# A hybrid decoder layer on one core: the down projection as seven products of halves

## The chip, the core and the metric

The kernel runs on one core of a Trainium2 chip. The core has five engines with queues of their own: TensorE (PE: matmuls, and weight loads, PEld), VectorE (DVE), ScalarE (ACT), GpSimd (POOL) and SyncE (SP), which issues the DMA transfers here. The metric is the device time of one execution in microseconds. The kernel before has a median of 2500.06 us over three runs (2499.16 to 2500.68).

## What is computed

One layer (DEPTH = 1) over 16 meta tokens and 1024 tokens, D_MODEL = 1024, all in float32: a token mixer (attention, a state-space mixer, gates), a norm, a gated MLP with a short convolution, and a last norm. The change touches only the end of the MLP:

```python
def conv_glu_ffn(h, w_up, conv_w, conv_b, w_down):
    u = causal_dwconv(h @ w_up, conv_w, conv_b)
    gate, val = jnp.split(u, 2, axis=-1)
    return (jax.nn.silu(gate) * val) @ w_down        # [1024 tokens, 2816] @ [2816, 1024]
...
ffn = conv_glu_ffn(h, w_up[i], ffn_conv_w[i], ffn_conv_b[i], w_down[i])
h = layer_norm(DEEPNORM_ALPHA * h + ffn, ln2_g[i], ln2_b[i])
```

## The kernel before

Every product of two float32 matrices is made of three float32r matmuls: `split` (L197) cuts a tile x into a high part H (a cast on ScalarE, L198) and a rest L (a subtraction on VectorE, L199), and H·H, L·H and H·L are added up in PSUM.

The kernel goes through its stages one after the other: embedding norm and latents, attention, output projections and gates, the state-space mixer, the mixer's output with the first norm, the up projection (L1083 to L1221), the down projection with the last norm (L1224 to L1308). The order on each queue is fixed when the kernel is built, by a planner that gives each engine the ready instruction that stands earliest in the program; `tc.high_priority(n)` lets instructions count as n places earlier (400 from L652 on). Tiles come from pools; a new tile waits until the tile whose place it takes is done with. SBUF is handed from stage to stage in this way, and each engine's queue runs in its order: an instruction that waits holds up all behind it.

Up projection (loop over f at L1178, 22 blocks of 128 hidden channels for gate and value): it already uses Strassen's seven products in Winograd's form, over halves of channels and of tokens. `wrest` (L1100) loads up weights (`wraw`), forms four sums s1 to s4 on GpSimd (L1107 to L1110) and splits them; `first` starts the next block's first product while the present one runs. Each product is 24 matmuls of 258 and 256 columns into a pair of banks (`dpair`). Results are combined on VectorE and ScalarE (L1191 to L1217), go through `conv_up` (L1127; `va`, `ga`, `gb` are its tiles, and two of its instructions, L1132, run on VectorE with two inputs), are multiplied and stored to DRAM as `gv_d[f]`, the second half of the tokens first (L1216, L1220).

Down projection: two halves r of 512 tokens. In each, `load_r` loads eight residual tiles `hr` and scales them on ScalarE (L1257, L1258), and the 22 channel blocks k go in groups (`KBLK`, L91: 2, 4, 4, 4, 4, 4). For each k `load_d` loads a whole row block of `w_down` (512 KB) into `wraw`, two buffers, and splits it into two column halves (`wh`, `wl`, 12 buffers of each); `load_g` loads `gv_d[k]` for this half of the tokens (256 KB) into `gv`, three buffers, and splits it into `dh` tiles, which have room for all of r. So `w_down` is loaded and split twice. Four token tiles t have two PSUM banks each, eight in all; the residual comes into PSUM by transposes with `ident` (L1296), ahead of the first group's matmuls. The matmuls of a group run tile by tile (L1305):

```python
for k in range(k0, k1):
    dhh, dhl = dh[k][0][:, o], dh[k][1][:, o]
    for i in range(3):
        for q in range(2):
            wh, wl = wd[k][q]
            a, b = ((dhh, wh), (dhl, wh), (dhh, wl))[i]
            nc.tensor.matmul(pss[q], a, b, start=False, stop=(k == NFF - 1 and i == 2))
if k1 == NFF:
    norm2(pss, 512 * r + P * t)
```

`norm2` (L1262) runs wholly on VectorE: `bn_stats` over the two banks (L1265), `bn_aggr` (L1267), nine small instructions for the inverse root (L234 to L239), then two instructions for each half (L1273, L1275), and two stores of `yt`.

## Time and profile before

| | us |
|---|---|
| median of three runs | 2500.06 |
| the profiled execution: its time | 2499.16 |
| its span, first to last instruction | 2497.2 |
| TensorE busy | 2412.9 (97%) |
| VectorE busy | 1675.0 (67%) |
| ScalarE busy | 1111.7 (45%) |
| GpSimd busy | 168.5 (7%) |
| last up matmul, first down matmul | 2224.43, 2236.82 |

Times in the trace count from the start of the span. Matmuls overlap in the pipeline, so the mean duration of one is longer than the step from one to the next; a step is found by dividing a full stretch by the matmuls in it. An idle time in brackets or behind a bar is that of the engine just before the instruction, with what ended it. The chain is followed back from the last instruction, at each step to what released it. The granted clock of TensorE has two levels, 2.4 GHz (1.00) and 1.2 GHz (0.50); a stretch's number is the mean.

### The profile page before, as it was taken

To read this page: it belongs to the slowest core of one execution; us is meant where nothing else is said; L and a number is where in the kernel's file an instruction comes from. 1 tells how busy PE (TensorE), PEld (TensorE's weight loads), DVE (VectorE), ACT (ScalarE), POOL (GpSimd) and SP (SyncE) were. 2 spreads that over 40 slices of the span, in tenths; PEclk is the share of its full clock that TensorE was granted. 3 is DMA by queue.
4 is the path that set the end of the run, shared out by engine and by line. 5 is a ranking of instruction groups with operands and counts; after the bars stand their busy time and mean duration, and the time that the engine had idled before them with its cause. 6 is when DMAs were issued, how large, how long until landed. Compare 5 with 4: busy or idle time off the path is not lost.

```text
span 2497.2 us, 42526 instructions
## 1 busy us (share of the span) xinstructions
PE 2412.9 (97%) x16451; PEld 2279.8 (91%) x16451; DVE 1675.0 (67%) x3834; ACT 1111.7 (45%) x2436; POOL 168.5 (7%) x168
## 2 busy tenths in 40 slices
PE   6999999999999999999999999999789999989998
PEld 6998898889999999999999999999789999987886
DVE  6467677774667777877777646746787777755624
ACT  6345455562245455545554323423544444445211
POOL 0000000000000000000000001001332222200000
PEclk9999999999999999999999999999899999999999
DMA  5121111152552212213222445534222222257421
GB/s 203 47 66 35 36 38 32 51 154 72 171 187 91 94 62 87 86 62 99 75 79 67 136 149 169 194 129 142 99 90 77 77 77 77 77 172 247 155 93 68
DMA packets 113530, 257.10 MB, mean 103 GB/s; under 512 B 13488, under 2 KB 48560, under 8 KB 111280
## 3 DMA queue, kind: packets, MB, share of 16 engines
q1 hardware_dynamic: 113328, 254.38, 31.3%
q8 instruction: 129, 2.11, 0.4%
q14 instruction: 73, 0.60, 0.1%
HBM read 200.97 MB, written 51.26 MB: 101 GB/s over the span
## 4 chain that ended last, share of the span: by engine, by line
PE 83%; DVE 7%; DMA 4%; ACT 2%; issue 1%; POOL 1%; SPq 0%; DVEq 0%; ACTq 0%; POOLq 0%
PE d L191 24%; PE g L171 12%; PE g L173 12%; PE g L172 12%; PE c L1305 7%; PE c L605 3%; PE c L880 2%; PE c L904 1%; PE c L599 1%; PE c L884 1%; DMA yl<-y_d 1%; DMA gv<-gv_d 1%; DVE f L199 1%; PE c L552 1%; PE c L554 1%
## 5 line engine op out<-in xcount | busy, mean ns | idle before, releaser
L191 PE MATMUL d<-f,wh 128*128 128x258 f32 (+1 forms) x4000 | 656.5, 287 | 22.6 <-ACT c L1159 5.8
L191 PEld LDWEIGHTS d<-f,wh 128*128 128x128 f32 x4000 | 560.5, 193 | 26.0 <-ACT c L1159 6.0
L171 PE MATMUL g<-h,wh 128*128 128x348 f32 (+3 forms) x1560 | 506.7, 325 | 4.0 <-ACT lat L387 4.0
L173 PE MATMUL g<-h,wh 128*128 128x348 f32 (+3 forms) x1560 | 505.6, 325 | 0.0
L172 PE MATMUL g<-h,wl 128*128 128x348 f32 (+3 forms) x1560 | 505.4, 324 | 0.0
L191 PE MATMUL d<-f,wl 128*128 128x258 f32 (+1 forms) x2000 | 407.0, 286 | 5.7 <-DVE wl L199 4.1
L191 PEld LDWEIGHTS d<-f,wl 128*128 128x128 f32 x2000 | 314.8, 193 | 7.2 <-DVE wl L199 5.0
L171 PEld LDWEIGHTS g<-h,wh 128*128 128x128 f32 x1560 | 293.9, 188 | 7.0 <-ACT lat L387 4.4
L161 DVE TENSOR_TENSOR wl<-wraw,wh 128x512 fp32r<-128x512 f32 (+2 forms) x278 | 192.4, 694 | 160.3 <-ACT wh L160 157.2
L172 PEld LDWEIGHTS g<-h,wl 128*128 128x128 f32 x1560 | 294.3, 189 | 2.5 <-issue 2.4
L173 PEld LDWEIGHTS g<-h,wh 128*128 128x128 f32 x1560 | 293.8, 188 | 2.4 <-issue 2.4
L160 ACT CAST wh<-wraw 128x512 fp32r<-128x512 f32 (+2 forms) x278 | 166.9, 604 | 251.7 <-PE d L191 119.0
L199 DVE TENSOR_TENSOR wl<-wraw,wh 128x512 fp32r<-128x512 f32 x154 | 111.5, 750 | 150.6 <-ACT wh L198 106.6
L1305 PE MATMUL c<-wh,dh 128*128 128x512 f32 x704 | 193.1, 396 | 9.4 <-ACT dh L198 8.4
L198 ACT CAST wh<-wraw 128x512 fp32r<-128x512 f32 x154 | 90.7, 618 | 221.5 <-PE c L1305 97.8
L1305 PEld LDWEIGHTS c<-wh,dh 128*128 128x128 f32 x704 | 132.4, 189 | 40.6 <-ACT dh L198 8.7
L171 PE MATMUL g<-a,wh 128*128 128x348 f32 (+2 forms) x456 | 149.2, 327 | 2.0 <-DVE kn L199 1.1
L172 PE MATMUL g<-a,wl 128*128 128x348 f32 (+2 forms) x456 | 147.8, 324 | 0.0
L173 PE MATMUL g<-a,wh 128*128 128x348 f32 (+2 forms) x456 | 147.7, 324 | 0.0
L785 DVE SCALAR_TENSOR_TENSOR xc<-g,V,xc 128x347 f32<-128x347 f32 (+2 forms) x180 | 103.7, 576 | 38.5 <-ACT xc L781 35.6
L870 ACT ACTIVATE G<-ac,tok 116x116 f32<-116x116 f32 x288 | 91.6, 379 | 42.7 <-PE c L880 42.7
L1305 PE MATMUL c<-wl,dh 128*128 128x512 f32 x352 | 109.9, 393 | 0.0
(270 smaller groups left out, 3897.8 us busy)
## 6 DMA issues: line engine op xcount, KB each, us to landing
wraw<-win SPq DMA_DIRECT2D x65, 512.0 KB, 3.4
wraw<-wup SPq DMA_DIRECT2D x48, 512.0 KB, 3.5
wraw<-wdl SPq DMA_DIRECT2D x44, 512.0 KB, 3.8
ac<-cs_d SPq DMA_DIRECT2D x16, 1044.0 KB, 5.7
wraw<-wos SPq DMA_DIRECT2D x32, 512.0 KB, 3.9
gv<-gv_d SPq DMA_DIRECT2D x44, 256.0 KB, 4.2
yl<-y_d SPq DMA_DIRECT2D x32, 257.0 KB, 3.5
wraw<-wout SPq DMA_DIRECT2D x16, 512.0 KB, 3.8
```

Of the source, the lines that this page charges most:

```text
L160: nc.scalar.copy(h[:, :n * ncol], r)
L161: nc.vector.tensor_sub(l[:, :n * ncol], r, f32(h[:, :n * ncol]))
L171: nc.tensor.matmul(ps, ah, bh, start=(k == 0), stop=False)
L172: nc.tensor.matmul(ps, al, bh, start=False, stop=False)
L173: nc.tensor.matmul(ps, ah, bl, start=False, stop=(k == n - 1))
L191: nc.tensor.matmul(ps[:, PO + c0:PO + c1], a, b[:, c0:c1], start=(start and k == 0 and i == 0), stop=(k == n - 1 and i == 2), skip_group_c ...
L198: nc.scalar.copy(H, src)
L199: nc.vector.tensor_sub(L, src, f32(H))
L605: nc.tensor.matmul(ops[:, o0:n], vt[j][:w, hh * P:(hh + 1) * P], ptt[:w, o0:n], start=(j == 0), stop=(j == nbmax - 1))
L785: nc.vector.scalar_tensor_tensor(t[:, l:n], ps[:, hal + l - s:hal + n - s], vec("cw", (3 - s) * 24 + ct), t[:, l:n], ALU.mult, ALU.add)
L870: nc.scalar.activation(G_[:, k * S:(k + 1) * S], ac[:S, hh, C0[b] + k * S:C0[b] + (k + 1) * S], AF.Relu, bias=tok[:, 3 * b + k, 32 + hd:33 ...
L1305: nc.tensor.matmul(pss[q], a, b, start=False, stop=(k == NFF - 1 and i == 2))
```

## The change

The down projection becomes seven products too. With A the 1024 tokens by 2816 channels cut into halves of tokens (first digit) and of channels (second), and B = `w_down` cut into halves of channels (`j` and `j + KH`, KH = 11) and of columns, each product is [512 x 1408] times [1408 x 512]: 11 channel blocks, four token tiles, three matmuls of 512 columns each.

- In the up projection `down_sums(j)` is called at the top of the passes f = 4 to 14. It loads two row blocks of `w_down` into `tw1` and `tw2` (one buffer each), forms the right operands of products 7, 5, 4 and 6 with four GpSimd subtractions in place, and stores them to DRAM (`t13_d`, `t42_d`). It has no priority of its own.
- In the down projection `left` gives the left operand: tiles of `gv_d`, loaded once and kept (`raw`, 4 tiles in pool `Ea`, 40 in `Eb`), or sums of them on GpSimd (11 for product 7, 22 for product 6, 11 for product 3). `right` loads a half row block (256 KB) of `w_down` or of a stored sum, two halves sharing one `wraw` tile. `forms` splits both; it has places for seven pairs at a time (4 in `Eh0` and `wp`, 3 in `Eh1` and `Ew`), and in the last product the last seven take places of `Eb`.
- The products go in the order 1, 2, 7, 6, 5, 3, 4, in groups of 4, 4, 3 blocks (the last one 4, 7), into four banks each. Between them results are copied out on ScalarE (`p1`, `u2`, `u4`) or added on VectorE.
- The residual is brought in by four calls of `residual` (four tiles each, 16 transposes), the first of them into banks of its own that ScalarE copies to `u4`.
- `norm2` runs on tiles of SBUF or PSUM. For a half in `pooled` the scaling is a ScalarE activation and two GpSimd instructions in place of two on VectorE: both halves of all tiles after product 3, one half of the first three tiles after product 4, none in the last tile.

```diff
+    t13_d = [dtile(f"t13_d{k}", [P, D]) for k in range(KH)]
+    t42_d = [dtile(f"t42_d{k}", [P, D]) for k in range(KH)]
...
+    def down_sums(j):
+
+        x, y = (pe[0].tile([P, D], F32, name=k, tag=k) for k in ("tw1", "tw2"))
+        nc.sync.dma_start(x, wdl[j])
+        nc.sync.dma_start(y, wdl[j + KH])
+        (b11, b12), (b21, b22) = ((t[:, :512], t[:, 512:]) for t in (x, y))
+        nc.gpsimd.tensor_sub(b11, b12, b11)
+        nc.gpsimd.tensor_sub(b12, b22, b12)
+        nc.gpsimd.tensor_sub(b22, b22, b11)
+        nc.gpsimd.tensor_sub(b21, b21, b22)
+        nc.sync.dma_start(t13_d[j], x)
+        nc.sync.dma_start(t42_d[j], y)
+
...
     for f in range(NFF):
         q = st[f]
+        if f >= NHEAD and f < NHEAD + KH:
+            down_sums(f - NHEAD)
...
+        def left(q, j):
+            if q in (1, 2, 4):
+                return A({1: 11, 2: 12, 4: 22}[q], j)
+            if q == 7:
+                t = p.tile([P, 512], F32, name="s3", tag="s3", bufs=3)
+                nc.gpsimd.tensor_sub(t, A(11, j), A(21, j))
+                return t
+            if q == 6:
+                nc.gpsimd.tensor_add(A(21, j), A(21, j), A(22, j))
+                nc.gpsimd.tensor_sub(A(11, j), A(21, j), A(11, j))
+                return A(11, j)
+            if q == 5:
+                return A(21, j)
+            nc.gpsimd.tensor_sub(A(12, j), A(12, j), A(11, j))
+            return A(12, j)
...
+        def forms(q, j, late):
             with tc.high_priority(wprio[0]):
...
+                n = count[0] % 7
+                res = []
+                for k, src in enumerate((left(q, j), right(q, j))):
+                    if late:
+                        hl = [pb.tile([P, 512], F32R, name="gv", tag="gv") for _ in range(2)]
+                    elif k == 0:
+                        hl = [(ph0 if n < 4 else ph1).tile([P, 512], F32R, name="dh", tag="dh") for _ in range(2)]
+                    else:
+                        pl, b = (wp, 4) if n < 4 else (p, 3)
+                        hl = [pl.tile([P, 512], F32R, name=t, tag=t, bufs=b) for t in ("wh", "wl")]
+                    split(*hl, src)
+                    res.append(hl)
+                count[0] += 1
+            return res
...
+        def product(q, pss, first, before=None, after=None):
+            blocks = ((0, 4), (4, KH)) if q == 4 else ((0, 4), (4, 8), (8, KH))
+            for k0, k1 in blocks:
+                fs = [forms(q, j, q == 4 and k0) for j in range(k0, k1)]
+                for t in range(4):
+                    o = slice(P * t, P * t + P)
+                    if k0 == 0 and before:
+                        before(t)
+                    for j, ((ah, al), (bh, bl)) in zip(range(k0, k1), fs):
+                        for i, (a, b) in enumerate(((ah, bh), (al, bh), (ah, bl))):
+                            nc.tensor.matmul(pss[t], a[:, o], b, start=(first and j == 0 and i == 0),
+                                             stop=(j == KH - 1 and i == 2), skip_group_check=not first)
+                    if k1 == KH and after:
+                        after(t)
...
+                if q in pooled:
+                    nc.scalar.activation(y, parts[q], AF.Identity, bias=nw, scale=rs)
+                    nc.gpsimd.tensor_tensor(y, y, g2[:, f], ALU.mult)
+                    nc.gpsimd.tensor_tensor(y, y, b2[:, f], ALU.add)
...
+        x0 = banks(gtile)
+        rp = banks(ctile)
+        add = residual(1, 1, rp, True)
+        for t in range(4):
+            add(t)
+            nc.scalar.copy(u4[t], rp[t])
+        product(1, x0, True, None, lambda t: nc.scalar.copy(p1[t], x0[t]))
...
+        product(2, x1, False, add, lambda t: nc.vector.tensor_add(p1[t], p1[t], x1[t]))
+        x2 = banks(ctile)
+        product(7, x2, True)
+        product(6, x0, False, None, lambda t: nc.scalar.copy(u2[t], x0[t]))
...
+        product(5, x0, False, None, c22)
+        add = residual(0, 1, x0, False)
+        product(3, x0, False, add, lambda t: norm2(0, t, (p1[t], x0[t]), (), (0, 1)))
+        add = residual(1, 0, x2, False)
...
+        product(4, x2, False, add, c21)
```

## Rows read from the trace of the kernel before

**Rows 1.** The page: busy time of TensorE; the chain's shares by engine.

```profile
PE 2412.9 (97%) x16451; PEld 2279.8 (91%) x16451; DVE 1675.0 (67%) x3834; ACT 1111.7 (45%) x2436; POOL 168.5 (7%) x168
...
PE 83%; DVE 7%; DMA 4%; ACT 2%; issue 1%; POOL 1%; SPq 0%; DVEq 0%; ACTq 0%; POOLq 0%
```

**Rows 2.** Stretches, from the up projection on: length, busy time per engine.

```profile
core 0: us, PE busy (x) PEld busy (x) DVE busy (x) ACT busy (x) POOL busy (x), PEclk, DMA share, GB/s
1782.00:1861.00 79.00, 66.43 (x481) 64.02 (x482) 63.41 (x80) 30.59 (x47) 28.64 (x20) 0.91 0.24 81
1861.00:2200.00 339.00, 338.94 (x2805) 338.59 (x2805) 260.96 (x339) 165.49 (x269) 88.28 (x64) 1.00 0.26 82
2224.50:2236.80 12.30, 3.87 (x35) 3.58 (x34) 6.68 (x12) 5.94 (x11) 0.00 (x0) 0.87 0.61 199
2236.80:2298.00 61.20, 60.23 (x253) 48.20 (x253) 30.84 (x48) 30.52 (x54) 0.00 (x0) 0.97 0.76 251
...
2374.00:2470.00 96.00, 96.00 (x420) 78.38 (x419) 20.71 (x32) 18.29 (x32) 0.00 (x0) 1.00 0.25 80
```

**Rows 3.** Groups by shape from 2224 on: busy us, mean ns | idle before.

```profile
L1305 PE MATMUL c<-wh,dh 128*128 128x512 f32 x704 | 193.1, 396 | 9.4 <-ACT dh L198 8.4 <-ACT wh L198 0.9
...
L199 DVE TENSOR_TENSOR wl<-wraw,wh 128x512 fp32r<-128x512 f32 x84 | 54.1, 688 | 98.0 <-ACT wh L198 54.0 <-PE c L1305 43.5
L198 ACT CAST wh<-wraw 128x512 fp32r<-128x512 f32 x84 | 47.9, 617 | 126.2 <-PE c L1305 97.8 <-DMA wraw<-wdl 27.4 <-DVE wl L199 0.9
```

**Rows 4.** TensorE's timeline at the seam: start, length, instructions [idle before].

```profile
2224.67 3.70 PE L1296 MATMUL c<-K,hr 128*128 128x128 f32 x32
2236.82 2.07 PE L1305 MATMUL c<-wh,dh 128*128 128x512 f32 x4 [8.45 <-ACT dh L198]
2238.69 1.05 PE L1305 MATMUL c<-wl,dh 128*128 128x512 f32 x2
```

**Rows 5.** The chain at the seam: start, length, what.

```profile
2228.37 0.70 DVE ga L1219
...
2230.49 4.97 DMA hr<-h_d
...
2235.57 0.63 ACT hr L1258
2236.20 0.58 ACT dh L198
```

**Rows 6.** GpSimd's groups, 1876 to 2200: first two of four, 63 operations together.

```profile
L1110 POOL TENSOR_TENSOR s<-wraw,s 128x512 f32<-128x512 f32 x16 | 25.9, 1621 | 1.3
L1107 POOL TENSOR_TENSOR s<-wraw 128x512 f32<-128x512 f32 x16 | 20.7, 1293 | 47.9 <-DVE wl L199 47.9
```

**Rows 7.** VectorE, 1876 to 2200: one line's min/median/max, then groups by shape.

```profile
L1132 DVE SCALAR_TENSOR_TENSOR va<-u,V,va x64: 743/941/1670, 1877.2 to 2191.9; 128x512 f32<-128x512 f32 x64
...
L1132 DVE SCALAR_TENSOR_TENSOR va<-u,V,va 128x512 f32<-128x512 f32 x64 | 71.2, 1113 | 15.3 <-ACT va L1130 14.2
...
L199 DVE TENSOR_TENSOR wl<-wraw,wh 128x512 fp32r<-128x512 f32 x48 | 41.7, 870 | 45.5 <-ACT wh L198 45.5
...
L1132 DVE SCALAR_TENSOR_TENSOR gb<-d,V,gb 128x512 f32<-128x512 f32 x32 | 24.0, 750 | 0.5
```

**Rows 8.** One tile's instructions: min/median/max ns, first and last start.

```profile
L700 SPq DMA_DIRECT2D xx<-dt_d x3: 450/478/482, 554.5 to 628.8; - x3
...
L684 ACT ACTIVATE ga<-g x24: 449/451/463, 569.4 to 717.2; 128x334 f32<-128x334 f32 x8, 128x348 f32<-128x348 f32 x8, 128x344 f32<-128x344 f32 x8
```

**Rows 9.** The page's DMA issues: count, size, median us to landing.

```profile
wraw<-wdl SPq DMA_DIRECT2D x44, 512.0 KB, 3.8
...
gv<-gv_d SPq DMA_DIRECT2D x44, 256.0 KB, 4.2
```

**Rows 10.** The chain at the end: start, length, what.

```profile
2482.27 1.22 DVE bs L1265 x2
...
2488.16 1.22 DVE bs L1265 x2
```

More of the change, by code (lines that the diff above doesn't have):

```diff
@@ L90 @@
 NHEAD = 4
-KBLK = ((0, 2), (2, 6), (6, 10), (10, 14), (14, 18), (18, 22))
+KH = NFF // 2
 G_ATT = 3
@@ new lines, in tile_hybrid, with A, right, residual @@
+    cut_psum(4)
+    with pool("Er", 4) as pr, pool("Ea", 4) as pa_, pool("Eh0", 8) as ph0, pool("Eb", 40) as pb, \
+            pool("Eh1", 6) as ph1, pool("Ew", 1) as p:
+        raw = {}
+        count = [0]
+        wr = [None]
+        def A(i, j):
+            if (i, j) not in raw:
+                t = raw[i, j] = (pa_ if i == 11 and j < 4 else pb).tile([P, 512], F32, name="gv", tag="gv")
+                o = 0 if i < 20 else 512
+                nc.sync.dma_start(t, gv_d[j + (KH if i % 10 == 2 else 0)][:, o:o + 512])
+            return raw[i, j]
+        def left(q, j):
[13 more added lines that the diff above has]
+            return A(12, j)
+        def right(q, j):
+            d, o = {1: (wdl[j], 0), 2: (wdl[j + KH], 0), 3: (wdl[j + KH], 512), 4: (t42_d[j], 0), 5: (t13_d[j], 0),
+                    6: (t42_d[j], 512), 7: (t13_d[j], 512)}[q]
+            if count[0] % 2 == 0:
+                wr[0] = wp.tile([P, D], F32, name="wraw", tag="wraw", bufs=2)
+            t = wr[0][:, 512 * (count[0] % 2):][:, :512]
+            nc.sync.dma_start(t, d[:, o:o + 512])
+            return t
+        def forms(q, j, late):
+            with tc.high_priority(wprio[0]):
+                n = count[0] % 7
[12 more added lines that the diff above has]
+            return res
+        def residual(hi, fh, pss, first):
+            with tc.high_priority(wprio[0]):
+                hr = []
+                for k in range(4):
@@ new lines, in residual @@
+            return lambda t: [nc.tensor.matmul(pss[t][:, k * P:k * P + P], hr[k][:, P * t:P * t + P], ident,
+                                               start=(first and k == 0), stop=(k == 3), is_transpose=True,
+                                               skip_group_check=not first) for k in range(4)]
+        def product(q, pss, first, before=None, after=None):
[12 more added lines that the diff above has]
+                        after(t)
@@ L1264, in norm2, with btile @@
+        def btile(name):
+            return [p.tile([P, 512], F32, name=name, tag=name, bufs=4) for _ in range(4)]
+        p1, u2, u4 = btile("p1"), btile("u2"), btile("u4")
+        bs = [[p.tile([P, 2, 6], F32, name="bs", tag="bs", bufs=8) for _ in range(4)] for _ in range(2)]
+        def norm2(hi, t, parts, have=(), pooled=()):
+            bt = bs[hi][t]
             for q in range(2):
-                nc.vector.bn_stats(bs[:, q], pss[q])
+                if q not in have:
+                    nc.vector.bn_stats(bt[:, q], parts[q])
@@ L1266, in norm2 @@
             mv = p.tile([P, 4], F32, name="mv", tag="mv", bufs=2)
[L1267 removed]
+            nc.vector.bn_aggr(mv[:, :2], bt.rearrange("p a b -> p (a b)"))
             rs, ve, nw = (p.tile([P, 1], F32, name=nm, tag=nm, bufs=2) for nm in ("rs", "ve", "nw"))
             rsqrt_col(rs, mv[:, 1:2], LN_EPS, ve, nw, P)
[L1270 to L1271 removed]
+            r0 = 512 * hi + P * t
@@ L1272, in norm2 @@
+            if pooled:
+                nc.vector.scalar_tensor_tensor(nw, mv[:, 0:1], -1.0, rs, ALU.mult, ALU.mult)
             for q in range(2):
-                nc.vector.scalar_tensor_tensor(yt[:, hv_[q]], pss[q], mv[:, 0:1], g2[:, hv_[q]], ALU.subtract, ALU.mult)
-            for q in range(2):
-                nc.vector.scalar_tensor_tensor(yt[:, hv_[q]], yt[:, hv_[q]], rs, b2[:, hv_[q]], ALU.mult, ALU.add)
-                nc.sync.dma_start(out[r0:r0 + P, hv_[q]], yt[:, hv_[q]])
+                f = slice(512 * q, 512 * q + 512)
+                y = p.tile([P, 512], F32, name="yt", tag="yt", bufs=3)
+                if q in pooled:
+                    nc.scalar.activation(y, parts[q], AF.Identity, bias=nw, scale=rs)
+                    nc.gpsimd.tensor_tensor(y, y, g2[:, f], ALU.mult)
+                    nc.gpsimd.tensor_tensor(y, y, b2[:, f], ALU.add)
+                else:
+                    nc.vector.scalar_tensor_tensor(y, parts[q], mv[:, 0:1], g2[:, f], ALU.subtract, ALU.mult)
+                    nc.vector.scalar_tensor_tensor(y, y, rs, b2[:, f], ALU.mult, ALU.add)
+                nc.sync.dma_start(out[r0:r0 + P, f], y)
@@ L1278, in tile_hybrid, with banks @@
+        def banks(tile_):
+            return [tile_() for _ in range(4)]
+        x0 = banks(gtile)
[5 more added lines that the diff above has]
+        product(1, x0, True, None, lambda t: nc.scalar.copy(p1[t], x0[t]))
         g2 = p.tile([P, D], F32, name="g2")
```

70 lines of the change are left out of this document (11 added, 59 removed).

## The prediction

> **What bounds the kernel now.** I read the page's busy shares and chain first [rows 1]: TensorE is busy 97% of the span and carries 83% of the chain, so the number of matmuls is the first thing to price. Then one table of stretches [rows 2], because an average over the whole span hides where TensorE waits. It shows four kinds of time. From 1782 to 1861 us (the first tiles of the up projection) TensorE is idle 12.6 of 79 us at a clock of 0.91 and VectorE is busy 80%: here other engines set the pace. From 1861 to 2200 TensorE is full, VectorE 77%, GpSimd 26%, DMA 26%. At the seam between up and down projection (2224.5 to 2236.8) TensorE does 3.87 us of work in 12.3. In the down projection it is full again: 420 matmuls in 96.00 us, 0.2286 us each. From 2236.8 to 2298 it runs only 253 where 61.2 us would hold 268, with the DMA at 0.76 of its time and 251 GB/s. The waits at the seam come from the chain and TensorE's timeline [rows 4, 5], the prices of single operations from the groups by shape [rows 3, 6, 7].
>
> **Matmuls removed.** Before: 2 halves x 4 tiles x 22 blocks x 3 x 2 = 1056 matmuls of 512 columns; the 704 with a high part as stationary operand are there [rows 3], and half as many have the rest. After: 7 products x 11 blocks x 4 tiles x 3 = 924 of the same shape (a 128x128 stationary piece of the left operand, 512 columns of weights moving, a new stationary load for each). 132 x 0.2286 = **-30.2 us**, all on the path. The transposes of the residual stay 64: four calls of 16.
>
> **The seam.** TensorE did its last up matmul and 32 transposes by 2228.4, then sat idle 8.45 us; the first matmuls after that went at half clock, 1.2 of 2.4 GHz (4 in 2.07, 2 in 1.05 us) [rows 4]. The chain [rows 5] says why: SyncE stood behind the store of the last up tile (L1219, L1220), then loaded residual for the second half (`hr`) before the first `gv` block, and ScalarE scaled that residual before it cut `dh`. Over 2236.8 to 2298 another (268 - 253) x 0.2286 = 3.4 us is lost, half clock included [rows 2]. The change holds four `gv` tiles in a pool of their own (`Ea`) beside four `hr` tiles, so the first block of four can be cut before the up projection ends, and gives 40 further tiles to the rest; the old stall of 8.45 + 3.4 = **-11.9 us** goes. What is late next: the `gv` loads no longer wait for one of three buffers. 40 x 256 KB = 10.5 MB become ready within some 15 us; at 251 GB/s for a share of 0.76, thus 330 GB/s for all of it, that is 32 us of transfer. Weight halves issued behind them wait. The first block covers 48 x 0.2286 = 11 us. A half behind a third of them takes 11 us instead of the 4.2 of such a load [rows 9] and is just covered; behind all, some 20 us are not. Bounds 0 and +20; I take **+5**, since half of these loads can run in the last 15 us of the up projection, where the DMA is at about a quarter.
>
> **Forms.** Each product needs 22 splits (11 left, 11 right): 22 x 0.617 = 13.6 us of ScalarE and 22 x 0.688 = 15.1 us of VectorE [rows 3] in 132 x 0.2286 = 30.2 us; 154 splits against 132 before. There is room on average; the tight place is the ring of seven forms. Where a block of four follows a block of four, the fourth form's buffers come free three matmuls into the last tile of the old block and are needed nine matmuls into the new: 9 + 9 matmuls, 4.1 us, for two casts and two subtractions (2.6 us in a row). That happens six times. Bounds: 0, and 2.3 us each (the chain hidden by almost nothing) = +14; I take **+4**, nearer to nothing, as 420 matmuls ran without a gap in the old ring [rows 2]. Copies out of PSUM wait for a bank used again at least 6 us later (nine matmuls for each of three tiles), so they lie beside matmuls.
>
> **Sums for the right operands.** 11 calls, each two 512 KB loads, four GpSimd operations, two 512 KB stores. GpSimd: 44 x 1.293 to 1.621 us [rows 6] = 57 to 71 us; its queue is 26% busy, so its own time is hidden. The transfers are 23 MB; over 140 us, the shortest that the calls can take (below), they add 165 GB/s to 82, which makes a share of 0.78, about what was reached at 251 GB/s [rows 2]. SyncE takes four more instructions a call, and a store waits for GpSimd with the loads of up weights queued behind it; those go a tile ahead, so I give that no price of its own. What isn't free is VectorE. Operations with two SBUF inputs grow beside GpSimd: `va` has 0.743 at best, 1.113 on average and 1.670 at worst, `wl<-wraw` 0.870 against 0.688, while `gb`, whose source is PSUM, stays at 0.750 [rows 3, 7]. 64 x 0.363 + 48 x 0.182 = 32.0 us for 63 GpSimd operations: 0.51 us each on average, at most 0.92. So 44 sums take 22 us of VectorE, at most 40.
>
> The Trainium skill (GPSIMD Engine Reference, 4.1 Engine selection) sends two-input elementwise work to VectorE, about twice as fast, and so speaks against these sums. The rows agree with the ratio (1.293 against 0.688); on VectorE they would cost it 30 us instead of 22, so little is won by the place, and the total would hardly change.
>
> Where they fall decides. A load written late in the program runs early when its engine is free: the `xx` loads of `dt_chain`, called after three `gate` calls, are issued at 554.5, before the first gate's result at 569.4 [rows 8]. So I expect the calls to run ahead, one per 13 us (3.8 load [rows 9], 5.5 sums, about 4 store), from 1782 on: six calls, 24 sums, before 1861, where VectorE is 80% busy and TensorE waits for it. 24 x 0.51 = 12 us, half of it on the path: **+6 us**. The other five fall where VectorE has 23% free. Bounds: 0 (all beside work) and 24 x 0.92 = +22. A gain is excluded: nothing of the up projection is removed.
>
> **The last norm.** Product 3's tiles are normed under product 4. In product 4 a tile comes each 21 x 0.2286 = 4.8 us; VectorE took 5.9 a tile before (2488.16 back to 2482.27) [rows 10] and now leaves two operations of 0.75 to ScalarE and GpSimd. The last tile stays on VectorE: one addition from PSUM more, one `bn_stats` less, then the old chain from 2488.16 on. Bounds -1 and +4 (a ring of three `yt` tiles held by a store); I take **+0.5**.
>
> **Sum.** -30.2 - 11.9 + 5 + 4 + 6 + 0.5 = -26.6. The profiled execution took 2499.16 us (span 2497.2), 0.9 below the median. 2499.16 - 26.6 + 0.9 = 2473.5; I round to **2473 us**.
>
> **Rivals.**
> (a) Everything hidden: the seam, the ring and the sums cost nothing. -42.1, so 2458 us. For it: TensorE without a gap from 1861 to 2200. Against: three new supplies would all have to be in time. Chance 0.14.
> (b) A starved start: the burst of `gv` loads delays the weights of the first products. Forecast + 15 = 2488 us. For it: 0.76 of the DMA in that stretch already with three buffers. Chance 0.12.
> (c) No change: the ring loses 1.5 us at each of its 19 block joints instead of 4 in all (28), beside the start: 2473 + 24 = 2497. Against: splits use half of VectorE's time. Chance 0.04.
> (d) Slower: GpSimd holds VectorE back. There are 110 new GpSimd operations: 44 sums in up, 44 left operands (11 + 22 + 11), 22 in the norms. At the worst loss seen, 0.92 us, that is 101 us of VectorE. It decides from the point where 46 of them (42 us) land on the path at that price; with two thirds of all, 67 us, the time is 2500 - 42 + 67 = 2525 us. Against it: in the down projection VectorE needs some 155 us (154 x 0.688 and about 50 for copies, statistics and norms) of 225, and 66 x 0.92 still fits. Chance 0.05.
> The Trainium skill (SBUF — State Buffer, Who interferes with whom) has the harder rule that the later of the two is blocked for a whole instruction; by it the sums before 1861 would cost 24 x 1.3 = 31 us, half on the path, and the time would be about 2483. That lies inside (b); the rows show 0.51, not 1.3, on average.
>
> **How the numbers follow.** Forecast 0.65, from 2463 to 2484; (a) 0.14, (b) 0.12, (c) 0.04, (d) 0.05. Leaving out (c), (d) and the far parts of (a) and (b), the range is 2456 to 2489. 0.2%, 5 us, is about what a measurement of this kernel can tell from no change: faster 0.91, same 0.04, slower 0.05.
>
> **What would show it.** Right: 924 matmuls of 512 columns at 0.229; TensorE's idle time at the seam below 3 us and no half clock there; GpSimd's sums beginning before 1800; `va` and `wl` longer before 1930. Wrong: TensorE waiting on `wh` or `wl` at every block (the ring), on `wraw` in the first two products (b), or GpSimd as the releaser of the casts in products 7 and 6, where 33 of its operations (43 us or more) feed 61 us of matmuls.

## The result, and the profile of the changed kernel

The changed kernel takes 2528.85 us (median of four runs, 2526.93 to 2531.04), the kernel before 2499.61 beside it: 1.0119 times as long, 95% interval 1.0101 to 1.0137. The forecast was 2473 us, so the prediction is wrong in sign: 29 us slower where 27 faster were expected. The profiled execution took 2531.04 us, its span is 2529.3, thus 32.1 more than before's.

First the page of the changed kernel: busy times and the chain's shares, as in [rows 1].

```profile
PE 2403.9 (95%) x16319; PEld 2269.6 (90%) x16319; DVE 1745.5 (69%) x3857; ACT 1136.7 (45%) x2481; POOL 336.8 (13%) x278
...
PE 78%; DVE 7%; POOL 4%; DMA 4%; issue 3%; ACT 2%; SPq 0%; DVEq 0%; POOLq 0%; ACTq 0%
```

TensorE has 132 matmuls less and 9 us less work, but it fills only 95% of the span, and GpSimd, with a seventh of TensorE's work, holds 4% of the chain where it had 1%. Cuts of the span at matmuls tell where the time went. The group `d<-f` of L191 has 6000 matmuls in either kernel, the mixer's output and then the up projection; its 2500th, at some 1775 us, comes early in the up projection and ahead of the first load of `down_sums`, which the changed kernel issues at 1781.5. The other cuts are the last of these 6000 and the first and last matmul of the down projection (before: L1305, after: L1321):

| us | before | changed | difference |
|---|---|---|---|
| start to the 2500th of the 6000 matmuls | 1775.6 | 1774.4 | -1.2 |
| from there to the last of them (up projection) | 449.0 | 485.3 | +36.3 |
| from there to the first down matmul | 12.3 | 5.5 | -6.8 |
| down projection, first to last matmul | 250.0 | 243.8 | -6.2 |
| last matmul to the end | 10.3 | 20.2 | +9.9 |

Together 32.1 us, within a rounding. Two stretches of the changed kernel's up projection, as in [rows 2], then the second of them in the kernel before:

```profile
1782.00:1861.00 79.00, 64.81 (x435) 61.77 (x436) 60.96 (x69) 26.51 (x43) 54.47 (x35) 0.85 0.55 191
1861.00:2000.00 139.00, 118.34 (x904) 116.95 (x903) 100.59 (x113) 52.17 (x87) 73.59 (x50) 0.93 0.47 165
...
1861.00:2000.00 139.00, 138.94 (x1150) 138.74 (x1150) 108.27 (x141) 68.27 (x111) 38.19 (x28) 1.00 0.25 80
```

The sums run from 1785 to 1957: they begin where it was foreseen, but a call takes 16 us instead of 13. Before 1861 TensorE runs 46 matmuls less than before (435 after 481 [rows 2]), after it 246 less (904 after 1150). At 139 / 1150 = 0.121 us each that is some 6 us and some 30. From 1861 to 2000 TensorE is idle 20.7 of 139 us and its clock falls to 0.93, where it was full before. No engine is full: VectorE has 72%, GpSimd 53%, the DMA 47%. GpSimd, ScalarE and VectorE wait for each other in turn and for loads, and the chain of that stretch (start, length, what) names them:

```profile
1880.73 0.32 SPq L1233
...
1881.15 5.24 DMA tw<-wdl
...
1886.52 1.73 POOL tw L1184
...
1889.62 1.74 POOL s L1109
1891.35 1.70 POOL tw L1186
1893.06 1.69 POOL s L1110
1894.75 1.25 POOL tw L1187
1896.00 1.26 POOL s L1112
1897.27 5.92 DMA wraw<-wup
...
1903.22 0.63 ACT wh L198
...
1904.48 1.76 DVE wl L199
...
1907.91 1.70 DVE va L1134
```

It is read from the bottom: VectorE waits for ScalarE's cast, that for an up weight (`wraw<-wup`). This load could not be issued before 1897.27, the moment in which `s4` (L1112) is done: `wraw` has two buffers, and GpSimd's sums are the last to read one. `s4` is late because in GpSimd's queue the sums of up weights (L1109 to L1112) stand between those of down weights (`tw`), and the first of these stood until its load, 5.24 us long, had landed. That load in turn stood on SyncE behind the store of `gb` (L1233), which waits for VectorE. Meanwhile TensorE ran out of weights.

The forms of the down projection: GpSimd's groups from 2290 to 2420, and the longest wait from 2300 to 2385 (total, times, longest).

```profile
L1264 POOL TENSOR_TENSOR gv<-gv 128x512 f32<-128x512 f32 x11 | 18.1, 1651 | 11.1 <-DMA gv<-gv_d 10.8
L1265 POOL TENSOR_TENSOR gv<-gv 128x512 f32<-128x512 f32 x11 | 17.9, 1640 | 0.4
L1269 POOL TENSOR_TENSOR gv<-gv 128x512 f32<-128x512 f32 x11 | 16.3, 1490 | 0.2
L1261 POOL TENSOR_TENSOR s<-gv 128x512 f32<-128x512 f32 x9 | 13.2, 1477 | 12.2 <-DVE dh L199 8.7 <-DMA gv<-gv_d 3.5
...
ACT dh L198 <- POOL s L1261: 34.8, 7, 12.2
```

Casts wait 34.8 us for product 7's sums (L1261): between them GpSimd has those of products 6 and 3 (L1264, L1265, L1269) in its queue, and each takes 1.48 to 1.65 us. Product 7 takes 46.3 us instead of 30.2.

And the end of the changed kernel: a group of VectorE after 2484, and two waits there.

```profile
L238 DVE SCALAR_TENSOR_TENSOR nw<-rs,ve 128x1 f32<-128x1 f32 x21 | 8.0, 388 | 0.5
...
ACT yt L1348 <- DVE nw L1343: 22.6, 4, 6.3
POOL yt L1349 <- ACT yt L1348: 10.5, 4, 3.3
```

The same group in the kernel before, from 2470 on:

```profile
L238 DVE SCALAR_TENSOR_TENSOR nw<-rs,ve 128x1 f32<-128x1 f32 x12 | 2.6, 220 | 0.4
```

The norms of product 3 are still under way when product 4's begin. VectorE's part grows beside GpSimd's, even the instructions on 128x1 (mean 388 ns after 220), and what is left to GpSimd waits for ScalarE, and ScalarE for VectorE.

### The profile page after: what moved, and what is told of

Read it like the earlier page. It is cut to its first block, busy times and chain, and to the rows that moved or that the text cites. A ratio compares the mean times of both kernels' runs of the same rounds, so it can differ in the third digit from the quotient of the medians.

```text
span 2529.3 us, 42622 instructions
## 1 busy us (share of the span) xinstructions
PE 2403.9 (95%) x16319; PEld 2269.6 (90%) x16319; DVE 1745.5 (69%) x3857; ACT 1136.7 (45%) x2481; POOL 336.8 (13%) x278
## 4 chain that ended last, share of the span: by engine, by line
PE 78%; DVE 7%; POOL 4%; DMA 4%; issue 3%; ACT 2%; SPq 0%; DVEq 0%; POOLq 0%; ACTq 0%
PE d L191 21%; PE g L171 12%; PE g L173 12%; PE g L172 12%; PE g L1321 5%; PE c L607 3%; PE c L882 2%; PE c L906 1%; PE c L601 1%; PE c L886 1%; DMA yl<-y_d 1%; DMA tw<-wdl 1%; DVE f L199 1%; PE c L554 1%; PE c L556 1%
## 5 line engine op out<-in xcount | busy, mean ns | idle before, releaser
L191 PE MATMUL d<-f,wh 128*128 128x258 f32 (+1 forms) x4000 | 666.5, 289 | 44.5 <-ACT u L1219 9.1
L191 PEld LDWEIGHTS d<-f,wh 128*128 128x128 f32 x4000 | 569.1, 196 | 49.6 <-ACT wh L198 10.3
L191 PE MATMUL d<-f,wl 128*128 128x258 f32 (+1 forms) x2000 | 412.0, 289 | 5.2 <-DVE wl L199 3.6
L191 PEld LDWEIGHTS d<-f,wl 128*128 128x128 f32 x2000 | 319.6, 196 | 6.6 <-DVE wl L199 4.4
L199 DVE TENSOR_TENSOR wl<-wraw,wh 128x512 fp32r<-128x512 f32 x136 | 119.0, 884 | 74.3 <-ACT wh L198 74.3
L198 ACT CAST wh<-wraw 128x512 fp32r<-128x512 f32 x136 | 82.4, 618 | 120.6 <-DMA wraw<-wup 60.5
L1134 DVE SCALAR_TENSOR_TENSOR va<-u,V,va 128x512 f32<-128x512 f32 x88 | 99.9, 1135 | 20.9 <-ACT va L1132 19.5
L1321 PE MATMUL g<-wh,dh 128*128 128x512 f32 x352 | 112.4, 401 | 1.5 <-ACT wh L198 1.5
```

The lines of the kernel that those rows point to most:

```text
L191: nc.tensor.matmul(ps[:, PO + c0:PO + c1], a, b[:, c0:c1], start=(start and k == 0 and i == 0), stop=(k == n - 1 and i == 2), skip_group_c ...
L198: nc.scalar.copy(H, src)
L199: nc.vector.tensor_sub(L, src, f32(H))
L1134: nc.vector.scalar_tensor_tensor(t, src[:, 2 - k:HN - k], vec("fw", (2 - k) * 44 + ti), t, ALU.mult, ALU.add)
L1321: nc.tensor.matmul(pss[t], a[:, o], b, start=(first and j == 0 and i == 0), stop=(j == KH - 1 and i == 2), skip_group_check=not first)
```

## The experiments

Three suspects, one for each loss; in the up projection also the question whether GpSimd's work, its traffic or its place in the queues costs the time. Lengths in this section come from one profile each, at the cuts of the table above; times of whole runs carry their intervals. The runs were taken in groups, with the kernel before beside each: 2497.57 us for n1 to n4, 2500.85 for n5 to n8, 2498.07 for n9 to n11, 2498.96 for n12. A difference of whole times across groups is uncertain by up to 3 us, so small ones rest on the lengths. Where an expectation gives the up projection 781, 817 or 827 us, it counts from the first of the 6000 matmuls; here it counts from the 2500th: 449.0 us before, 485.3 in the changed kernel.

### The up projection

**n1_down_alone** leaves out the sums of the down weights; the products that took them take raw halves.

```diff
-            down_sums(f - NHEAD)
...
-            d, o = {... 4: (t42_d[j], 0), 5: (t13_d[j], 0), 6: (t42_d[j], 512), 7: (t13_d[j], 512)}[q]
+            d, o = {... 4: (wdl[j + KH], 0), 5: (wdl[j], 0), 6: (wdl[j + KH], 512), 7: (wdl[j], 512)}[q]
```

> Left out: all of down_sums (no loads, no GpSimd subtractions, no stores of the 11 pairs); the four products that took sums of down weights take raw halves of w_down instead, in the same loads of the same size, so the output is not the reference's. Everything else is the change: seven products with their left-operand sums on GpSimd, and the last norm. Both theories of the up projection (the queues that SyncE and GpSimd share, or the port that GpSimd and VectorE share) expect the up projection to end where it did before, at 2224 us of the span (after: 2260), so 36 us sooner, and a time near 2529 - 36 = 2493 us. A third theory, that the two up-projection losses are due to something else in the change (other placement of the buffers, another order from the planner), expects an end of the up projection above 2240. Seam, product 7 (46 us) and the tail of 20 us after the last matmul stay as in the changed kernel if those losses have nothing to do with the sums of the down weights.

Measured: 2496.18 us, 0.9992 of the kernel before (0.998 to 1.0005). The up projection takes 448.6 us and ends at 2226.5. Product 7 (46.1) and the end (19.9) are as in the changed kernel. So all of the 36 us come from `down_sums`, and the rest of the change, with 30 us of matmuls removed, gains nothing by itself.

**n2_sums_no_dma** keeps the 44 GpSimd operations, on one resident pair of tiles, and leaves out the other loads and the stores. It also holds each group of four behind the `s4` of the block's up weights.

```diff
+            if f == NHEAD:
+                with tc.issue_after(st[f - 1]["ga"]):
+                    tw = down_loads(0)
+            with tc.issue_after(st[f]["s4"]):
+                down_sums(*tw)
```

> Left out: the loads of w_down into tw and the stores of the sums, except one pair of loads; the 11 x 4 GpSimd subtractions run as in the change, but on one resident pair of tiles, each group right behind that pass's own sum s4 on GpSimd. The products of the down projection take raw halves of w_down, so the output is not the reference's. It keeps GpSimd's work (44 operations of 1.2 to 1.7 us) and takes away its traffic. Port theory (a GpSimd operation that reads on-chip memory holds VectorE's operations back, 0.5 to 0.9 us for each): 44 x 0.5 to 0.9 = 22 to 40 us of VectorE in a stretch where it has 25 us to spare, so an end of the up projection at 2235 to 2260 us. Queue theory (loads of up weights wait on SyncE behind stores that wait for GpSimd; GpSimd waits for loads): end at 2224 to 2232 us, time near 2493 to 2500.

Measured: 2505.15 us (1.0028, 1.0016 to 1.004); up projection 457.5 us, end at 2232.8, between the two theories' numbers. Its chain decides: the 8.5 us are lost between the 3000th and the 3500th matmul, where the only call with loads stands and two more run close behind it.

```profile
1868.44 4.79 DMA tw<-wdl
...
1873.30 1.19 POOL tw L1186
...
1882.32 1.26 POOL s L1112
1883.59 3.45 DMA wraw<-wup
```

A `tw` load, GpSimd's queue, `s4`, an up weight. From the 3500th matmul on, with most calls still to come, 2000 matmuls take 242.2 us against 241.5 before. So GpSimd's work as such was not the cause of the 36 us.

**n3_dma_no_sums** keeps the 22 loads and 22 stores where the planner had put them and leaves out the four subtractions.

```diff
-        nc.gpsimd.tensor_sub(b11, b12, b11)
-        nc.gpsimd.tensor_sub(b12, b22, b12)
-        nc.gpsimd.tensor_sub(b22, b22, b11)
-        nc.gpsimd.tensor_sub(b21, b21, b22)
```

> Left out: the four GpSimd subtractions of each down_sums; its two loads and two stores stay, placed by the planner as in the change, so t13 and t42 hold raw halves and the output is not the reference's. It keeps the traffic (22 loads and 22 stores of 0.5 MB) and takes GpSimd's work away. Queue theory with GpSimd as a link of it (stores wait for sums, up-weight loads wait behind stores): without the sums a store waits only for its load, 4 us, so about half of the 36 us goes, an end of the up projection at 2235 to 2250 us. Theory that the traffic alone does it: end at 2255 to 2260 as in the changed kernel. Port theory: end at 2224 to 2230, as nothing is left of its cause.

Measured: 2502.52 us (1.0022, 1.0009 to 1.0034); up projection 455.4 us, end at 2234.9, the lower edge of what the queue theory gave. The traffic alone, bunched as it is without sums between, costs 6.4 us; the stretch where it falls:

```profile
1782.00:1861.00 79.00, 64.38 (x452) 61.79 (x451) 58.29 (x81) 32.87 (x52) 23.62 (x17) 0.88 0.70 236
```

The DMA works at 0.70 there (before: 0.24, [rows 2]). 8.5 us by the sums (one call's loads among them) and 6.4 by the traffic make 15 of 36; the rest needs both.

**n4_paced** holds the change to one call per pass: loads behind the `gv` store of the pass before, stores behind that of the own pass.

```diff
+            with tc.issue_after(st[f - 1]["ga"]):
+                tw = down_loads(f - NHEAD)
+            down_sums(*tw)
...
+            with tc.issue_after(st[f]["ga"]):
+                nc.sync.dma_start(t13_d[f - NHEAD], tw[0])
+                nc.sync.dma_start(t42_d[f - NHEAD], tw[1])
```

> Nothing left out. The order of issue alone is changed: the loads of a down_sums call are issued behind the last store of the pass before, its two stores behind the last store of its own pass, one call in each of 11 passes of the up projection, so no load of up weights stands on SyncE behind a store that still waits for GpSimd. Queue theory: the up projection ends at 2226 to 2235 us, 25 to 34 us sooner than in the changed kernel, and the time is 2495 to 2504 us. Port theory: the same 44 operations hold VectorE back as before, spread over 11 passes: end at 2245 to 2260 us, time above 2514 us.

Measured: 2543.29 us (1.0176, 1.0148 to 1.0204), slower than the changed kernel; up projection 494.3 us. The queue theory missed, and the port theory had the time (above 2514) but not the end of the up projection (2245 to 2260; measured 2273). I held SyncE's stores ahead of up-weight loads for the link. With these put right a pass still took some 24 us instead of 20, and the chain of one pass shows the whole ring:

```profile
1897.16 3.60 DMA t_d<-tw
1900.78 3.56 DMA tw<-wdl
...
1904.47 1.29 POOL tw L1186
1905.76 1.71 POOL s L1109
...
1907.54 1.63 POOL s L1110
...
1909.25 1.30 POOL s L1112
1910.57 3.40 DMA wraw<-wup
```

The next call's load waits for the store of the call before (`tw1` and `tw2` have one buffer each), the first `tw` sum waits for that load, `s1` to `s4` stand behind this sum on GpSimd, and the next up weights behind `s4`. The pacing, which ties the stores to the end of a pass on VectorE, made every pass go through this.

**n9_after_s4** differs from n4 in the place of the sums: traced a pass later and held behind the `s4` formed in that pass (that of the next block), so they start a pass after their loads were issued.

```diff
+            with tc.issue_after(st[f + 1]["s4"]):
+                down_sums(*tw)
+            with tc.issue_after(st[f - 1]["ga"]):
+                nc.sync.dma_start(t13_d[j - 1], tw[0])
+                nc.sync.dma_start(t42_d[j - 1], tw[1])
...
+            with tc.issue_after(st[f - 1]["ga"]):
+                tw = down_loads(j)
```

> Nothing left out. As the paced kernel before it, but GpSimd's four sums of a call stand behind the four sums of up weights of their pass (s4 last), a whole pass after their loads were issued, so GpSimd never stands waiting for a tw load with sums of up weights queued behind it; stores and the next loads follow the pass's gv store on SyncE. If the loss of the up projection comes from that chain (store of tw, load of tw, GpSimd's sum, s1 to s4, load of up weights), it falls from 35 us in the changed kernel and 46 in the paced one to the 8 to 10 us that the sums alone and the traffic alone cost, at most their total of 17: up projection 789 to 799 us long (before 781, changed 817, paced 827), time 2503 to 2513 us. If GpSimd's work itself were the price of the up projection, 810 us or longer and 2524 us or more.

Measured: 2499.91 us (1.0004, 0.9995 to 1.0014), below the range expected, and 43 less than n4 with the same operations and the same transfers; up projection 451.9 us, and 448.6 and 449.1 in two later kernels with the same code in it (n12, n10). GpSimd's timeline of one pass:

```profile
1916.93 1.29 POOL L1109 TENSOR_TENSOR s<-wraw 128x512 f32<-128x512 f32 x1 [2.69 <-DVE wl L199]
1918.30 1.29 POOL L1110 TENSOR_TENSOR s<-s,wraw 128x512 f32<-128x512 f32 x1
1919.67 1.62 POOL L1112 TENSOR_TENSOR s<-wraw,s 128x512 f32<-128x512 f32 x1
1921.26 1.74 POOL L1186 TENSOR_TENSOR tw<-tw 128x512 f32<-128x512 f32 x1
```

No `tw` sum waits for a load, and `s1`, `s2` and `s4` follow each other. The place of the `tw` sums in GpSimd's queue, ahead of `s4` and close behind their own loads, is shown to be the cause. The place behind `s4` and the age of the loads were changed together; no run has one without the other.

### The down projection

The seven products in the order in which they run, first matmul to next first matmul. 132 x 0.2286 = 30.2 us; products 2, 3 and 4 have 16 transposes inside, at 32 in 3.70 us [rows 4] another 1.85. Products 5, 3 and 4 are 30.9, 32.3 and 31.5 in all the runs of the table.

| us | up | 1 | 2 | 7 | 6 | last matmul to the end |
|---|---|---|---|---|---|---|
| changed | 485.3 | 35.5 | 36.9 | 46.3 | 30.6 | 20.2 |
| n5 left sums on VectorE | 483.8 | 34.5 | 44.1 | 33.5 | 30.6 | 20.4 |
| n6 norm on VectorE | 484.7 | 35.6 | 37.0 | 46.4 | 30.6 | 12.9 |
| n7 both | 486.2 | 33.4 | 46.6 | 33.1 | 30.6 | 12.8 |
| n11 both, banks drained first | 485.6 | 35.0 | 31.9 | 30.7 | 30.6 | 13.1 |
| n9 | 451.9 | 34.9 | 38.5 | 46.7 | 30.6 | 20.3 |
| n12 = n9, other order on GpSimd | 448.6 | 35.4 | 32.2 | 31.1 | 52.6 | 20.4 |
| n8 = n4 and n7 | 494.8 | 34.8 | 46.9 | 32.3 | 30.6 | 13.1 |
| n10 = n9 and n11 | 449.1 | 35.1 | 31.9 | 30.7 | 30.6 | 13.0 |

**n5_left_vector**

```diff
-                nc.gpsimd.tensor_sub(t, A(11, j), A(21, j))
+                nc.vector.tensor_sub(t, A(11, j), A(21, j))
...
-                nc.gpsimd.tensor_add(A(21, j), A(21, j), A(22, j))
-                nc.gpsimd.tensor_sub(A(11, j), A(21, j), A(11, j))
+                nc.vector.tensor_add(A(21, j), A(21, j), A(22, j))
+                nc.vector.tensor_sub(A(11, j), A(21, j), A(11, j))
```

(and product 3's sum likewise.)

> Nothing left out. The 66 sums of the left operand in the down projection (A11-A21, A21+A22 and so on, 128x512, 1.2 to 1.7 us each on GpSimd) move to VectorE; the rest is the changed kernel. Theory that GpSimd is what product 7 waits for: product 7 falls from 46.3 to 31 to 34 us and the stall of 5 us ahead of it goes, 14 to 20 us in all, time 2509 to 2515 us. Rival, that the products wait for their weight loads: product 7 stays above 42 us and the time stays within 4 us of 2529. Rival, that VectorE is full there (it is busy 46 of 60 us between 2300 and 2360): the stalls move to VectorE and no more than 6 us are gained.

The expectation says 66 sums; there are 44. Measured: 2523.79 us (1.0095, 1.0073 to 1.0117), 5 less than the changed kernel, not 14 to 20. Product 7 falls to 33.5 as expected of a GpSimd-bound one, but product 2 with the stall behind it grows to 44.1. That is the number of the expectation's last rival (VectorE full, 6 us at most), but n11 below has the same sums on VectorE without the stall.

**n7_left_norm_vector** has the edits of n5 and n6 together.

> Nothing left out. Both of the two before at once: left-operand sums and the norm's GpSimd part on VectorE, so the down projection leaves GpSimd idle. If the two losses are separate, their gains add: 14 to 20 plus 7 to 10 us, time 2500 to 2508 us. If VectorE becomes the bound of the down projection, less than the larger of the two alone.

Measured: 2517.63 us (1.0072, 1.0053 to 1.0092); the two gains of 5 add to 11, short of what was expected of them. What TensorE waits for now: the wait ahead of product 7, then the chain up to it.

```profile
PE c L1321 <- DVE p L1373: 14.6, 1, 14.6
...
2341.49 1.20 DVE s L1261 x2
2342.70 1.81 DVE gv L1264 x3
2344.51 2.41 DVE gv L1265 x4
2346.91 1.20 DVE gv L1264 x2
2348.12 1.20 DVE gv L1265 x2
2349.32 0.61 DVE p L1373
```

Product 7 uses the banks of product 2, and the addition that drains the last of them (L1373, `p1 += x1`) stands on VectorE behind 13 sums that count as 400 places earlier. The changed kernel has the wait in a smaller size: 4.8 us on the same addition, behind subtractions that wait for GpSimd's sums.

**n11_down_evac** is n7 with that addition set ahead.

```diff
+        def c11_(t):
+            with tc.high_priority(600):
+                nc.vector.tensor_add(p1[t], p1[t], x1[t])
```

> Nothing left out. The changed kernel with left-operand sums and norm on VectorE, and the add that drains product 2's banks (p1 += x1) set ahead of the sums of product 6 on VectorE. With the sums on VectorE the stall of 15.0 us ahead of product 7 was TensorE waiting for that add, which stood behind 13 sums of product 6. If that is so, the stall falls to 1 to 4 us and the time is 11 to 14 us below the same kernel without it: 2504 to 2507 us. If the weight loads are what product 7 waits for after all, the stall stays above 10 us and the time within 3 us of 2518.

Measured: 2503.32 us (1.002, 1.0009 to 1.0032), 14.3 less than n7 (12 if each is taken against the kernel before beside it). The stall is gone; products 2, 7 and 6 take 31.9, 30.7 and 30.6, their matmuls and transposes alone but for 0.5 us.

**n12_pool_order** asks whether the sums could have stayed on GpSimd: n9, with the sums of product 6 held behind the last one of product 7.

```diff
+                raw["s7"] = nc.gpsimd.tensor_sub(t, A(11, j), A(21, j)).ins
...
+                with tc.issue_after(raw["s7"]):
+                    nc.gpsimd.tensor_add(A(21, j), A(21, j), A(22, j))
+                    nc.gpsimd.tensor_sub(A(11, j), A(21, j), A(11, j))
```

> Nothing left out. The kernel with GpSimd's sums of down weights behind s4, all else as in the changed kernel (left-operand sums on GpSimd, norm partly on GpSimd), and one more rule for GpSimd's order: the 22 sums of product 6 stand behind the eleventh and last sum of product 7. It tells GpSimd's speed from its order in product 7 (46.7 us long without this rule, 30.2 for its matmuls alone). Order: product 7 falls to 30 to 35 us, product 6 stays at 31 to 34, time 2484 to 2492 us. Speed (11 + 22 sums at 1.3 to 1.7 us need 43 to 56 us): what product 7 gains is lost in product 6, which grows to 36 us or more, and the time is 2493 to 2502 us.

Measured: 2498.47 us (1.0001, 0.999 to 1.0012). Product 7 falls from 46.7 to 31.1 us and product 6 rises from 30.6 to 52.6. From the first matmul of product 2 to the end of product 6 it is 115.9 us in n9 and here, against 93.2 in n10. These are the numbers that the expectation gave for GpSimd's speed. Two groups and three waits of n12, then its chain ahead of the longest wait of TensorE:

```profile
L1273 POOL TENSOR_TENSOR gv<-gv 128x512 f32<-128x512 f32 x11 | 18.8, 1741 | 0.0
L1274 POOL TENSOR_TENSOR gv<-gv 128x512 f32<-128x512 f32 x11 | 17.9, 1654 | 0.0
...
POOL s L1269 <- DVE dh L199: 39.6, 6, 31.2
ACT gv L198 <- POOL gv L1278: 18.0, 1, 18.0
PE g L1330 <- ACT wh L198: 12.1, 1, 12.1
...
2341.82 5.06 POOL gv L1274 x3
...
2348.07 8.59 POOL gv L1278 x7
...
2357.30 0.52 ACT dh L198
```

The numbers fit, but the trace does not show that speed is the cause. The 22 sums take 36.7 us without an idle moment, more than product 7 covers, yet they are done in time: those of the first eight blocks at 2336.7, all at 2346.9. TensorE stands in its eighth block from 2346.3 to 2358.4, because ScalarE has a cast for product 4's last forms in its queue ahead of that block's, and that cast waits 18.0 us for product 3's sums (L1278). And earlier, among product 7's sums, GpSimd stood still for 31.2 us in one piece, because no `s3` tile was free. So order on GpSimd decided product 7, order on ScalarE cost product 6 at least 12.1 us, and whether the sums could stay on GpSimd in a better order, or with more `s3` tiles, stays open.

**n6_norm_vector**

```diff
-        product(3, x0, False, add, lambda t: norm2(0, t, (p1[t], x0[t]), (), (0, 1)))
+        product(3, x0, False, add, lambda t: norm2(0, t, (p1[t], x0[t]), (), ()))
...
-            norm2(1, t, (u2[t], u4[t]), (1,), (1,) if t < 3 else ())
+            norm2(1, t, (u2[t], u4[t]), (1,), ())
```

> Nothing left out. The part of the last norm that the change gave to GpSimd goes back to VectorE; the products and the sums of weights are those of the changed kernel. Theory that GpSimd's norm makes the tail long (20.0 us from the last matmul to the end, 9.9 before): tail of 10 to 13 us, time 2519 to 2522 us. Rival, that the tail is long because the norm of earlier tiles comes late, behind the seven late forms' own work on VectorE: tail of 18 to 24 us, time 2527 to 2533 us.

Measured: 2523.67 us (1.0097, 1.0079 to 1.0114), 5 less than the changed kernel and 1.7 above the range expected, and an end of 12.9 us instead of 20.2, inside it. So 7.3 of the 9.9 us are the norm's place on GpSimd; the remaining 2.6 stay in every run with the norm on VectorE, and no run takes them apart.

### Together

**n8_all** is n4 and n7.

> Nothing left out. The order of issue of the sums of down weights held to one call in each pass, and left-operand sums and norm on VectorE. If the queue theory, the GpSimd-bound product 7 and the GpSimd norm are each right, the gains add, 25 to 34 in the up projection plus 21 to 30 in the down projection: 2465 to 2483 us, faster than the kernel before. If the port theory holds for the up projection, 2495 to 2508 us.

Measured: 2529.1 us (1.0121, 1.0098 to 1.0145): 14 less than n4, where n7 gave 11; neither range of the expectation came, since n4's pacing was the wrong cure and lengthened the up projection to 494.8 us.

**n10_all_s4_evac** is n9 and n11.

> Nothing left out. Both together: GpSimd's sums of down weights behind s4 of their pass, left-operand sums and norm on VectorE, and product 2's draining add ahead of the sums of product 6. If the three causes are separate, the gains add: 18 to 26 us in the up projection, 23 to 26 us behind it, from 2529: 2477 to 2488 us, 0.5 to 0.9 per cent faster than the kernel before. If they only trade places with other waits, 2495 us or more.

Measured: 2468.49 us, 0.9879 of the kernel before (0.9864 to 0.9894), faster than both kernels and 60 us below the changed one. More than expected: the up projection lost nothing at all (449.1 us), and what lies behind it is 28.7 us shorter than in the changed kernel, where 23 to 26 were expected. From its page, a stretch of it, and a group of VectorE from 1876 to 2200:

```profile
PE 80%; DVE 9%; DMA 4%; ACT 2%; issue 2%; POOL 1%; SPq 0%; DVEq 0%; ACTq 0%; POOLq 0%
...
1861.00:2200.00 339.00, 338.88 (x2796) 337.95 (x2795) 275.14 (x337) 165.14 (x269) 156.76 (x108) 1.00 0.44 148
...
L199 DVE TENSOR_TENSOR wl<-wraw,wh 128x512 fp32r<-128x512 f32 x49 | 52.3, 1068 | 34.4 <-ACT wh L198 34.4
```

All 44 sums of the change and their transfers lie in this stretch, and TensorE is idle 0.12 us of 339. VectorE pays 275.14 - 260.96 [rows 2] = 14.2 us, 0.32 per sum, and TensorE doesn't wait for it.

## Why the prediction was wrong

Term by term, in us; "changed" against before at the cuts of the first table, and n10 the same way, where the change's matmuls run without its three faults. A product's surplus is its length less 30.2, or less 32.05 where transposes are inside; the 3.4 of the old start are gone, as the new one is counted from 30.2.

| term | forecast (bounds) | changed | n10 |
|---|---|---|---|
| matmuls removed | -30.2 | -30.2 | -30.2 |
| old stall at the seam, slow old start | -8.5 - 3.4 | -6.8 - 3.4 | -7.3 - 3.4 |
| start of product 1 | +5 (0 to +20) | 35.5 - 30.2 = +5.3 | +4.9 |
| ring of forms, products 2 to 4 | +4 (0 to +14) | +21.8 | +1.2 |
| sums, in the up projection | +6 (0 to +22) | +36.3 | +0.1 |
| last norm, end | +0.5 (-1 to +4) | +9.9 | +2.7 |

- **Matmuls and seam: right.** 924 matmuls; products 7, 6 and 5 take 30.6 to 30.9 us in n10. At the seam the changed kernel's TensorE waits 2.51 us before the transposes, below the 3 us foretold, and the stretch is 6.8 us shorter. The sign "no half clock there" did not come: the clock is 0.68 from 2265.3 to 2267.5 and 0.93 over product 1. The start cost what was taken for it, and rival (b) did not come.
- **The sums: the step that failed first.** Where the sums begin was right (1785), their pace was not: five calls instead of six begin before 1861, and the last ends at 1957. The 6 us were put on the path before 1861 and nothing behind it; lost were some 6 us before and some 30 behind, so that the first number fits by luck. The price was taken from the wrong resource. I wrote "a store waits for GpSimd with the loads of up weights queued behind it; those go a tile ahead, so I give that no price of its own", and that GpSimd's own time was hidden since its queue is 26% busy. A busy share says nothing of an engine that stands still at the head of its queue: there `s1` to `s4` wait behind a `tw` sum, and the loads of up weights wait for `s4`, because `wraw` has two buffers. These loads were not a tile ahead of GpSimd but on its heels: the load of 1897.27 starts when `s4` (1896.00, 1.26 long) ends. With the sums behind `s4` and their loads a pass old the price is next to nothing (448.6 to 451.9 us in n9, n12 and n10, against 449.0). n4, my first cure, moved SyncE's stores and made it worse; n9 leaves them where n4 put them and loses next to nothing, so they alone were not the link. That the single `tw` buffer closes the ring is read from n4's chain; no run has two.
- **VectorE's price: right mechanism, too large.** 44 x 0.51 = 22 us were put on VectorE; n10 shows 14.2, all beside TensorE's work.
- **The ring: the left sums had no price.** The term was worked out for ScalarE's and VectorE's splits, and these do fit, +1.2 us in n10. GpSimd's 33 sums for products 7 and 6 stood only in the last paragraph, as 43 us that feed 61 us of matmuls: 33 x 1.3. That paragraph named the sign by which the prediction would be wrong, and the sign came: GpSimd releases the casts of product 7 (34.8 us). The sums take 1.62 to 1.74 us each beside VectorE (n12), 17.7 + 18.8 + 17.9 = 54.4 us, and they were not spread over the 61: in the changed kernel product 7's stand among those of products 6 and 3, and three `s3` tiles hold them to the splits. Against the same sums on VectorE, with the draining addition ahead, this costs 115.9 - 93.2 = 22.7 us (n9, n10). How much of it is GpSimd's speed and how much the order of the queues is not shown.
- **The norm: bounds too narrow.** I bounded it by a held `yt` tile, and counted instructions per tile of VectorE. Beside GpSimd's two instructions for a half VectorE's are slower, the tiny ones too (0.22 to 0.39 us on average; 0.21 in n6, which has none on GpSimd), and product 3's norms run into product 4's.
- **Rival (d), 2525 us, had the number and not the cause.** It put the loss on VectorE, held back by GpSimd. In n10 VectorE is held back by the same 44 sums while TensorE loses nothing, and in the down projection casts waited for GpSimd itself. It was to decide from 46 operations on the path by VectorE. In the changed kernel's chain from 1782 to 1966 there are 11 of VectorE that took 1.46 to 1.79 us, some 10 us more than at their usual 0.69 to 0.75: a part of the loss, but not the 42 us.

The Trainium skill (GPSIMD Engine Reference, 4.1 Engine selection) sends two-input elementwise work to VectorE as about twice as fast. I wrote that the total would hardly change by it. For the sums of down weights that holds: on GpSimd, behind `s4`, they are free. For the left operands, as they were queued here, it does not: 0.685 us on VectorE (n7) against 1.62 to 1.74 (n12), and 23 us of the time between n9 and n10.

What the 2.6 us at the end are stays open; no run changes them.

## What to carry to other kernels

Before work goes to an idle engine, follow what already stands in its queue: who waits for that work, how far ahead its inputs are, and what happens if the new instruction waits there for a load. Place new work behind the last instruction that others wait for, with its inputs a full pass old, and let the drain of a shared bank go ahead of work for a later stage. A busy share bounds how much an engine can do, not how late it delivers.

## What the runs showed of the hardware that was not expected

- A GpSimd operation of two 128x512 inputs has two lengths, about 1.29 us and 1.6 to 1.8. In n9 from 1862 to 2200 all 49 long ones overlap work of VectorE with two SBUF inputs, but so do 39 of the 58 short ones. So both engines pay, though not each time. The Trainium skill (SBUF — State Buffer, Who interferes with whom) calls their shared port pair an exclusive lock, for which a VectorE instruction with two SBUF inputs contends with a GpSimd instruction that reads SBUF. It says that the later one is blocked for the whole instruction where it speaks of VectorE's two-port modes; the prediction took that for these operations too. Single operations do grow nearly that far: `wl` took 1.76 us in the changed kernel's chain, 0.688 before [rows 3]. On average over n10's stretch it was 0.32 us per sum.
- The growth does not fall on all VectorE work: beside 44 sums `wl<-wraw` went from 0.870 [rows 7] to 1.068 us, and `va`, the most stretched before, stayed (1.113 [rows 7], 1.075 in n10).
- The granted clock was 0.93 from 1861 to 2000 in the changed kernel, where TensorE was idle 20.7 us, and 1.00 before and in n10. The 904 matmuls there were busy 118.3 us, 0.131 each, against 0.121 before (138.9 for 1150): some 9 us beside the idle 20.7, so part of what a stall costs comes in the matmuls after it.
